# A head's transposes in one row with the weighted sum of one head and the scores of another

## The chip, the cores and the metric

The kernel runs on one core of one Trainium2 chip. The metric is the device time of one execution in microseconds (us). Its engines are PE (TensorE: matmuls, with PEld for its weight loads), DVE (VectorE), ACT (ScalarE), POOL (GpSimd) and SP (SyncE, which only issues transfers here). Each takes its own instructions in the order in which they were written for it.

## The reference, cut to what matters

Two layers. Each has four token mixers, three of them attention with four heads of 64, then gates and branch projections, an output projection and a squared-ReLU MLP. The part around the change:

```
h = rms_norm(x, g_mix)
(a_q, a_k, a_v, b_qlat, ..., c_f, d_val, d_gate) = split(h @ w_in)
out_a = chunk_band_attention(a_q, a_k, a_v, rel_bias)          # 4 heads
out_b = block_causal_attention(q, k, v, CHUNK)                 # 4 heads
out_c = block_causal_attention(c_q, c_k, c_v, 1, f_cum)        # 4 heads
out_d = silu(layer_norm(conv(d_val * sigmoid(d_gate))))
proj  = einsum('bsnc,ncd->bsnd', branches, w_branch)
gates = sigmoid(h @ w_gate + b_gate).reshape(b, s, 4, D_MODEL)
x = x + sum(gates * proj, axis=2) @ w_o
x = x + square(relu(rms_norm(x) @ w_up)) @ w_down
```

256 tokens, width 1024, everything in float32. A head's attention is softmax(q k + bias) v.

## The kernel before

Every float32 weight tile (128 x 1024, 512 KB) is loaded by SP, cast to a high part on ACT (`hi`, line 114) and its rest is taken on DVE or POOL (`lo`, line 115); a product is then three matmuls (lines 122 to 124: high by high, low by high, high by low). One such tile against 256 tokens is 24 matmuls of 256 columns. DVE, ACT and POOL get their order from a scheduler; PE's order is that in which the code is written (line 86).

The twelve heads of a layer (mixer A heads 0 to 3, B 4 to 7, C 8 to 11) are not a stage of their own. Their pieces stand between weight tiles of the projections and the gates: `mtile` ends in `tick()`, and each tick takes the next list of `side` and runs it. For PE a head has three pieces. `scores` (S, line 555) is two products of 128 and 256 columns in plain float32; heads of mixer A have a stationary operand of 64 rows, those of B and C of 128. `transposes` (pT, line 582) turns the three 128 x 128 blocks of the normalised probabilities, which ACT copies out as `pts`. `weighted` (pPV, lines 593 and 594) is again 256 and 128 columns, with a stationary operand of 64 columns. A piece of another kind in this stretch is `pf` (lines 471 and 472, the forget sums), with the columns of an S. The profile shows each plain float32 matmul twice, as two passes.

In `plan` head i has its scores at tick 4 + 2i, its transposes three ticks and its weighted sum four ticks after them. So even ticks hold a weighted sum and a scores, odd ticks a transposes alone. The ticks go on through the projections (0 to 12) into the loop over the 16 gate groups, `gates(g)`, of two tiles (two ticks) each. While `side` still holds a list, that loop does nothing but gates, and every second `lo` goes to POOL (`share[1] = 2`). The first group at whose end `side` is empty takes `conv_silu` and `sigmoids(0)`; each group behind it is followed by one `branch(m)`, and what is left of the eight branches stands behind the last group.

A branch is one weight tile, 24 matmuls of 0.12 us, into two banks of PSUM (`pbr`); DVE multiplies each by the gates (`yt`, line 737), POOL adds in two steps (lines 738 and 739), ACT casts the sum to `yh` (line 740) and DVE takes the rest `yl` (line 741). Behind the branches comes the output projection: four accumulators `po`, in the same four banks that `pgt` and `pbr` go round in, six matmuls each per weight tile and pair of banks, in the order po[0,0], po[1,0] (first tile), po[0,1], po[1,1] (second tile).

Of the kernel before, what the change touches and what calls it, by code (L numbers as in the profile page):

```python
# [47 lines left out]
A0 = 4  # L48
# [22 lines left out]
def hybrid_trunk(ctx: ExitStack, tc: tile.TileContext, xT, xtok, pos, small, gfin, abias, w_lat, w_v, w_in, w_uq, w_ukv,  # L71
# [253 lines left out]
    for l in range(L):  # L325
# [346 lines left out]
            tick()  # L672


        NH = 3 * HEADS
        NT = A0 + 2 * NH + 3
        plan = [[] for _ in range(NT)]
        for i in range(NH):
            plan[A0 + 2 * i].append((2, scores, i))
            plan[A0 + 2 * i + 3].append((1, transposes, i))  # L680
            plan[A0 + 2 * i + 4].append((0, weighted, i))
        side = [[(lambda f=f, i=i: f(i)) for _, f, i in sorted(p, key=lambda e: e[0])] for p in plan]
        side[0].append(lambda: latents(share[2]))
        if l == 0:
# [283 lines left out]
```

## Time and profile before

| what | value |
|---|---|
| median of 3 runs | 844.85 us (843.68 to 844.89) |
| profiled execution, span | 845.43 us, 843.6 us |
| granted PE clock over the span | 0.996 of full |
| busy PE, DVE, ACT, POOL | 826.0, 569.9, 450.0, 152.7 us |
| chain that ended last | PE 89%, DVE 5%, issue 2%, POOL 1%, ACT 1% |
| L114 ACT cast `hi`, mean | 1024 ns |

Busy time says how long an engine had an instruction in it; the chain follows the last instruction back to what released each step. A PE start is a better measure than a PE duration, since matmuls overlap: the starts of gate matmuls stand 0.12 us apart while each lasts 0.28 us.

### The profile page before, as it was taken

To read this page: it belongs to the slowest core of one execution; us is meant where nothing else is said; L and a number is where in the kernel's file an instruction comes from. 1 tells how busy PE (TensorE), PEld (TensorE's weight loads), DVE (VectorE), ACT (ScalarE), POOL (GpSimd) and SP (SyncE) were. 2 spreads that over 40 slices of the span, in tenths; PEclk is the share of its full clock that TensorE was granted. 3 is DMA by queue.
4 is the path that set the end of the run, shared out by engine and by line. 5 is a ranking of instruction groups with operands and counts; after the bars stand their busy time and mean duration, and the time that the engine had idled before them with its cause. 6 is when DMAs were issued, how large, how long until landed. Compare 5 with 4: busy or idle time off the path is not lost.

```text
span 843.6 us, 14520 instructions
## 1 busy us (share of the span) xinstructions
PE 826.0 (98%) x5646; PEld 759.5 (90%) x5646; DVE 569.9 (68%) x950; ACT 450.0 (53%) x759; POOL 152.7 (18%) x156
## 2 busy tenths in 40 slices
PE   9989999999999999999999999999999999999996
PEld 8969999999889999999899899999998899999994
DVE  7889984787665555555578899557866655555554
ACT  6745646654464444544485764485445554545443
POOL 6524332124200000000004332312331000000000
PEclk9999999999999999999999999999999999999999
DMA  8655433555546555555554544345555555555531
GB/s 281 232 181 181 132 126 126 166 184 185 165 164 198 189 189 186 186 189 187 172 176 161 188 132 145 132 131 174 194 176 200 175 186 190 191 185 186 188 126 50
DMA packets 42549, 145.55 MB, mean 173 GB/s; under 512 B 5104, under 2 KB 7408, under 8 KB 42352
## 3 DMA queue, kind: packets, MB, share of 16 engines
q1 hardware_dynamic: 41904, 142.98, 52.1%
q10 hardware_dynamic: 576, 1.64, 0.5%
q8 instruction: 44, 0.72, 0.4%
q14 instruction: 25, 0.20, 0.1%
HBM read 143.55 MB, written 1.05 MB: 171 GB/s over the span
## 4 chain that ended last, share of the span: by engine, by line
PE 89%; DVE 5%; issue 2%; POOL 1%; ACT 1%; DMA 0%; SPq 0%; POOLq 0%; DVEq 0%; ACTq 0%
PE pgt L122 7%; PE pgt L123 7%; PE pgt L124 7%; PE pu L123 7%; PE pu L124 7%; PE pu L122 7%; PE pd L123 7%; PE pd L122 7%; PE pd L124 7%; PE S L555 2%; DVE lo L115 2%; PE pqk L122 2%; PE pPV L593 2%; PE pqk L123 2%; PE pqk L124 2%
## 5 line engine op out<-in xcount | busy, mean ns | idle before, releaser
L115 DVE TENSOR_TENSOR lo<-raw,hi 128x1024 fp32r<-128x1024 f32 (+3 forms) x241 | 300.5, 1250 | 195.9 <-ACT hi L114 193.9
L114 ACT CAST hi<-raw 128x1024 fp32r<-128x1024 f32 (+2 forms) x273 | 278.5, 1024 | 266.0 <-issue 208.0
L122 PE MATMUL pgt<-xgh,hi 128*128 128x256 f32 x512 | 149.5, 292 | 0.0
L122 PE MATMUL pu<-xgh,hi 128*128 128x256 f32 x512 | 144.9, 283 | 0.7 <-ACT xgh L293 0.7
L123 PE MATMUL pu<-xgl,hi 128*128 128x256 f32 x512 | 145.1, 283 | 0.3
L124 PE MATMUL pu<-xgh,lo 128*128 128x256 f32 x512 | 144.9, 283 | 0.0
L123 PE MATMUL pgt<-xgl,hi 128*128 128x256 f32 x512 | 144.7, 283 | 0.0
L124 PE MATMUL pgt<-xgh,lo 128*128 128x256 f32 x512 | 144.7, 283 | 0.0
L122 PE MATMUL pd<-hi,u 128*128 128x512 f32 x256 | 100.8, 394 | 1.6 <-ACT u L803 1.6
L123 PE MATMUL pd<-hi,u 128*128 128x512 f32 x256 | 100.7, 393 | 1.1 <-DVE u L804 1.1
L122 PEld LDWEIGHTS pu<-xgh,hi 128*128 128x128 f32 x512 | 98.0, 191 | 3.4 <-ACT xgh L293 1.1
L123 PEld LDWEIGHTS pu<-xgl,hi 128*128 128x128 f32 x512 | 98.0, 191 | 3.0 <-DVE xgl L294 0.7
L124 PE MATMUL pd<-lo,u 128*128 128x512 f32 x256 | 99.6, 389 | 0.0
L122 PEld LDWEIGHTS pgt<-xgh,hi 128*128 128x128 f32 x512 | 97.9, 191 | 0.8 <-issue 0.3
L123 PEld LDWEIGHTS pgt<-xgl,hi 128*128 128x128 f32 x512 | 98.1, 192 | 0.4
L124 PEld LDWEIGHTS pu<-xgh,lo 128*128 128x128 f32 x512 | 98.0, 191 | 0.0
L124 PEld LDWEIGHTS pgt<-xgh,lo 128*128 128x128 f32 x512 | 97.9, 191 | 0.0
L115 POOL TENSOR_TENSOR lo<-raw,hi 128x1024 fp32r<-128x1024 f32 (+1 forms) x32 | 77.4, 2419 | 111.2 <-ACT hi L114 106.5
L491 DVE SCALAR_TENSOR_TENSOR cacc<-up,sm,cacc 128x256 f32<-128x256 f32 x120 | 77.9, 693 | 0.0
L122 PEld LDWEIGHTS pd<-hi,u 128*128 128x128 f32 x256 | 48.3, 189 | 10.8 <-ACT u L803 2.4
L124 PEld LDWEIGHTS pd<-lo,u 128*128 128x128 f32 x256 | 48.1, 188 | 10.4
L123 PEld LDWEIGHTS pd<-hi,u 128*128 128x128 f32 x256 | 48.3, 189 | 9.7 <-DVE u L804 2.0
(255 smaller groups left out, 1358.3 us busy)
## 6 DMA issues: line engine op xcount, KB each, us to landing
raw<-in_w_gate SPq DMA_DIRECT2D x64, 512.0 KB, 3.7
raw<-in_w_up SPq DMA_DIRECT2D x64, 512.0 KB, 4.2
raw<-in_w_dn SPq DMA_DIRECT2D x64, 512.0 KB, 4.2
raw<-in_w_in SPq DMA_DIRECT2D x23, 512.0 KB, 4.2
raw<-in_w_br SPq DMA_DIRECT2D x16, 512.0 KB, 3.7
raw<-in_w_o SPq DMA_DIRECT2D x16, 512.0 KB, 4.3
raw<-in_w_v SPq DMA_DIRECT2D x8, 512.0 KB, 4.2
raw<-in_w_lat SPq DMA_DIRECT2D x8, 210.0 KB, 4.6
```

The source lines that it names most:

```text
L114: cut = nc.scalar.copy(hi[:, c:c + w], raw[:, c:c + w])
L115: done = eng.tensor_tensor(lo[:, c:c + w], raw[:, c:c + w], hi[:, c:c + w], op=ALU.subtract)
L122: nc.tensor.matmul(ps, sh, mh, start=first, stop=False)
L123: nc.tensor.matmul(ps, *((sl, mh) if late_mov else (sh, ml)), start=False, stop=False)
L124: nc.tensor.matmul(ps, *((sh, ml) if late_mov else (sl, mh)), start=False, stop=last)
L491: ins = nc.vector.scalar_tensor_tensor(cacc[:, c, :], up[:, c, j:j + T], wcol, cacc[:, c, :], op0=ALU.mult, op1=ALU.add)
L555: nc.tensor.matmul(sl, q[:, b * P:(b + 1) * P], k[:, 0:n], start=True, stop=True)
L593: nc.tensor.matmul(po[o:o + 64, 0:T], v[:, 0, vo:vo + HD], pts[:, 0:T], start=True, stop=False)
```

## The change

The transposes of a head move from three to four ticks behind its scores, and its weighted sum from four to six. Both are now on even ticks; within a tick the sum of head i stands first, then the transposes of head i + 1, then the scores of head i + 3. The list of ticks is two longer.

```
         NH = 3 * HEADS
-        NT = A0 + 2 * NH + 3
+        NT = A0 + 2 * NH + 5
         plan = [[] for _ in range(NT)]
         for i in range(NH):
             plan[A0 + 2 * i].append((2, scores, i))
-            plan[A0 + 2 * i + 3].append((1, transposes, i))
-            plan[A0 + 2 * i + 4].append((0, weighted, i))
+            plan[A0 + 2 * i + 4].append((1, transposes, i))
+            plan[A0 + 2 * i + 6].append((0, weighted, i))
```

On PE, in the first layer among the gates, before (the numbers tell the heads' tiles apart; left out are the gate matmuls between):

```order
L582 MATMUL pT_1234<-ident,pe_1083 128x128 x3
...
L593 MATMUL pPV_1273<-pts_1238,VB_383 64x256
L594 MATMUL pPV_1273<-pts_1238,VB_383 64x128
L555 MATMUL S_1276<-qkB_380 128x128
L555 MATMUL S_1276<-qkB_380 128x256
```

and now, the same head's sum and its successor's transposes:

```order
L593 MATMUL pPV_1355<-pts_1271,VB_383 64x256
L594 MATMUL pPV_1355<-pts_1271,VB_383 64x128
L582 MATMUL pT_1358<-ident,pe_1187 128x128 x3
L555 MATMUL S_1364<-qkB_380 128x128
L555 MATMUL S_1364<-qkB_380 128x256
```

Three transposes have moved from between two weight tiles into the row of the sum and the scores.

On DVE, at the end of the first layer's branches, before (yt_2524 is branch 5, yt_2629 branch 6, yt_2672 branch 7, Z_1099<-pgt_2561 the last gates, lo_2713 and on the weights of the output projection):

```order
L741 TENSOR_TENSOR yl_1992<-yt_2524,yh_1991 128x256
L115 TENSOR_TENSOR lo_2713<-raw_2711,hi_2712 128x1024
L717 TENSOR_TENSOR Z_1099<-pgt_2561,rb_465 128x512
L115 TENSOR_TENSOR lo_2731<-raw_2729,hi_2730 128x1024
L737 TENSOR_TENSOR yt_2629<-pbr_2630,Z_1099 128x512
L737 TENSOR_TENSOR yt_2629<-pbr_2644,Z_1099 128x512
L115 TENSOR_TENSOR lo_2749<-raw_2747,hi_2748 128x1024
L741 TENSOR_TENSOR yl_1992<-yt_2629,yh_1991 128x256
L737 TENSOR_TENSOR yt_2672<-pbr_2673,Z_1099 128x512
L737 TENSOR_TENSOR yt_2672<-pbr_2687,Z_1099 128x512
L115 TENSOR_TENSOR lo_2767<-raw_2765,hi_2766 128x1024
L741 TENSOR_TENSOR yl_1992<-yt_2672,yh_1991 128x256
```

and now (yt_2586 is branch 5, yt_2629 and yt_2672 branches 6 and 7 again, Z_1096<-pgt_2518 the last gates):

```order
L718 TENSOR_TENSOR Z_1096<-pgt_2518,rb_465 128x512
L115 TENSOR_TENSOR lo_2713<-raw_2711,hi_2712 128x1024
L738 TENSOR_TENSOR yt_2586<-pbr_2587,Z_1096 128x512
L738 TENSOR_TENSOR yt_2586<-pbr_2601,Z_1096 128x512
L115 TENSOR_TENSOR lo_2731<-raw_2729,hi_2730 128x1024
L742 TENSOR_TENSOR yl_2054<-yt_2586,yh_2053 128x256
L738 TENSOR_TENSOR yt_2629<-pbr_2630,Z_1096 128x512
L738 TENSOR_TENSOR yt_2629<-pbr_2644,Z_1096 128x512
L115 TENSOR_TENSOR lo_2749<-raw_2747,hi_2748 128x1024
L738 TENSOR_TENSOR yt_2672<-pbr_2673,Z_1096 128x512
L742 TENSOR_TENSOR yl_2054<-yt_2629,yh_2053 128x256
L738 TENSOR_TENSOR yt_2672<-pbr_2687,Z_1096 128x512
```

With two ticks more, the first branch stands one gate group later, and behind the last group there are now three branches (5, 6, 7) where there were two (6, 7).

## Rows read from the trace of the kernel before

**Rows 1.** Page, busy us, share and instructions of each engine.

```profile
PE 826.0 (98%) x5646; PEld 759.5 (90%) x5646; DVE 569.9 (68%) x950; ACT 450.0 (53%) x759; POOL 152.7 (18%) x156
```

**Rows 2.** Busy time in a stretch: from:to, length, then each engine.

```profile
80.00:200.00 120.00, 120.00 (x950) 114.86 (x950) 90.99 (x162) 68.61 (x127) 34.41 (x22) 1.00 0.48 152
```

**Rows 3.** PE's waits: us in total, times, longest.

```profile
PE po L122 <- DVE yt L737: 0.6, 2, 0.3
```

**Rows 4.** Timeline of PE, gates, first layer: start us, us, engine line op.

```profile
91.06 0.28 PE L124 MATMUL pgt<-xgh,lo 128*128 128x256 f32 x1
91.27 0.65 PE L593 MATMUL pPV<-pts,VAC 128*64 128x256 f32 x2
...
92.06 0.92 PE L555 MATMUL S<-qkB 128*128 128x128 f32 x4
...
92.94 0.28 PE L123 MATMUL pgt<-xgl,hi 128*128 128x256 f32 x1
...
95.57 0.28 PE L124 MATMUL pgt<-xgh,lo 128*128 128x256 f32 x1
95.69 0.49 PE L582 MATMUL pT<-ident,pe 128*128 128x128 f32 x3
...
96.14 0.28 PE L123 MATMUL pgt<-xgl,hi 128*128 128x256 f32 x1
```

**Rows 5.** Timeline of PE, transposes with the forget sums behind them.

```profile
87.20 0.28 PE L124 MATMUL pgt<-xgh,lo 128*128 128x256 f32 x1
87.32 0.49 PE L582 MATMUL pT<-ident,pe 128*128 128x128 f32 x3
...
88.42 0.28 PE L123 MATMUL pgt<-xgl,hi 128*128 128x256 f32 x1
```

**Rows 6.** Timeline of PE, the gate matmuls around a weighted sum alone.

```profile
153.41 0.28 PE L124 MATMUL pgt<-xgh,lo 128*128 128x256 f32 x1
...
154.64 0.28 PE L123 MATMUL pgt<-xgl,hi 128*128 128x256 f32 x1
```

**Rows 7.** Timeline of PE, mixer A: scores alone, then around sum and scores.

```profile
58.34 0.39 PE L124 MATMUL pv<-lo,xgh 128*128 128x512 f32 x1
58.66 0.92 PE L555 MATMUL S<-qkA 64*128 64x128 f32 x4
...
59.84 0.39 PE L123 MATMUL pv<-hi,xgl 128*128 128x512 f32 x1
...
74.79 0.28 PE L124 MATMUL pqk<-xgh,lo 128*128 128x256 f32 x1
...
76.87 0.28 PE L123 MATMUL pqk<-xgl,hi 128*128 128x256 f32 x1
```

**Rows 8.** Timeline of DVE at the last two branches, first layer.

```profile
215.06 1.28 DVE L737 TENSOR_TENSOR yt<-pbr,Z 128x512 f32<-128x512 f32 x2
216.25 1.21 DVE L115 TENSOR_TENSOR lo<-raw,hi 128x1024 fp32r<-128x1024 f32 x1
219.91 0.43 DVE L741 TENSOR_TENSOR yl<-yt,yh 128x256 fp32r<-128x256 f32 x1 [2.45 <-ACT yh L740]
220.26 1.28 DVE L737 TENSOR_TENSOR yt<-pbr,Z 128x512 f32<-128x512 f32 x2
```

**Rows 9.** Timeline of POOL and ACT, branch 6, first layer.

```profile
216.48 2.14 POOL L738 TENSOR_TENSOR yt<-yt 128x512 f32<-128x512 f32 x1 [5.72 <-DVE yt L737]
218.69 0.75 POOL L739 TENSOR_TENSOR yt<-yt 128x256 f32<-128x256 f32 x1
219.47 0.41 ACT L740 CAST yh<-yt 128x256 fp32r<-128x256 f32 x1 [3.31 <-POOL yt L739]
```

**Rows 10.** Timeline of PE, start of the output projection, first layer.

```profile
217.86 0.40 PE L122 MATMUL po<-hi,yh 128*128 128x512 f32 x1
...
220.38 0.39 PE L124 MATMUL po<-lo,yh 128*128 128x512 f32 x1
221.09 0.47 PE L122 MATMUL po<-hi,yh 128*128 128x512 f32 x1 [0.31 <-DVE yt L737]
```

## The prediction

> **What bounds the kernel now.** I read the busy times first: PE is busy for 826.0 of 843.6 us [rows 1]. Then the stretch in which the heads' pieces stand among the gates: from 80 to 200 us PE is busy for all of 120 us at a granted clock of 1.00, while DVE has 91 and ACT 69 [rows 2]. So a piece of a head costs there what it takes on PE, and what other engines do more or later costs nothing until PE waits for it. Then the list of PE's waits: between the heads and the MLP it has one row, 0.6 us in two waits, one in each layer, where the output projection waits for DVE's products of the last branch [rows 3]. The change touches both: what PE does at the ticks, and how many branches stand in front of the output projection. The sum has these two terms.
>
> **PE at the ticks.** I price a place by the starts of the weight matmuls around it: from the last line 124 before it to the first line 123 behind it, less the two starts that would be there anyway. Gate matmuls start 0.12 us apart (92.94 to 95.57 is 22 starts, 2.63 us) [rows 4].
> - Transposes alone: 96.14 - 95.57 - 0.24 = 0.33 us [rows 4]. They start 0.12 behind the gate matmul, like another gate matmul: the place has no hole at its front.
> - Sum and scores (mixers B, C): 92.94 - 91.06 - 0.24 = 1.64 us [rows 4].
> - Sum alone: 154.64 - 153.41 - 0.24 = 0.99 us [rows 6]. So scores behind a sum add 0.65.
> - Transposes and forget sums: 88.42 - 87.20 - 0.24 = 0.98 us [rows 5]; behind transposes, the same columns as a scores add 0.98 - 0.33 = 0.65 too.
>
> Sum and scores have the same columns, and yet a sum alone takes 0.99 and a scores 0.65. The 0.34 more is the sum's own: its first pass starts 0.21 behind a gate matmul instead of 0.12 (91.06 to 91.27) [rows 4], and the rest, some 0.2 to 0.25, lies behind it. It is there whether a scores or a gate matmul comes next, since the difference of the two places is just the scores. Transposes have the 128 x 128 form of both, so I expect the same hole in front of them and none behind: sum, transposes and scores in a row take 1.64 + 0.33 = 1.97 us, what the two places take now. For the 11 sums per layer that get transposes behind them that is a gain of 0. No row shows transposes behind a sum, so the bounds are these: they fill the hole (-0.2 each, 22 times: -4.4 us) or meet a second one on the way to the scores (+4.4 us). I take 0, since the rows on either side of the new place, sum with scores and transposes with forget sums, both add up without gain or loss.
>
> Mixer A's scores are another form, 64 rows. Alone between matmuls of 512 columns, which start 0.23 apart, such a scores takes 59.84 - 58.34 - 0.46 = 1.04 us, and it starts 0.32 behind its predecessor: holes of its own on both sides [rows 7]. Sum and scores of mixer A together take 76.87 - 74.79 - 0.24 = 1.84 us [rows 7], less than 0.99 + 1.04 = 2.03: the hole between the two odd forms is paid once. Heads 2 and 3 stand behind a sum now. After the change head 2's scores stand behind transposes, and head 3's behind sum and transposes: the shared hole, 0.19 us, is paid separately at both. Two heads, two layers: 4 x 0.19 = +0.8 us. Bounds: 0, if the hole in front of such a scores is not there behind transposes, and 1.2 us with 0.3 each, the whole 0.32 of that start.
>
> The Trainium skill, TensorE: Matmul & The Clock Gate, Part 3 (The mechanism), says that a weight load runs beside matmuls in flight only if its row group differs. The rows differ: loads of full height are busy for 90% of the span beside PE's 98% [rows 1], and it is the 64-row scores that starts late [rows 7]. By the page mixer A's term would be 0 and the sum 1.9 us in place of 2.7.
>
> The two added ticks cost PE nothing by themselves, as the same gate tiles are only counted against other lists. One more `lo` per layer goes to POOL and leaves DVE; PE waits for neither in that stretch. Transposes now stand a tick further behind their scores and sums two ticks behind their transposes, so both find their operands earlier than now.
>
> **The end of the branches.** DVE goes strictly down its list: the products of one branch wait behind `yl` of the branch before, which waits for ACT's cast, which waits for POOL's two adds. From one branch's products to the next that is 220.26 - 215.06 = 5.20 us [rows 8], made of 1.28 for the products, 2.14 and 0.75 on POOL, 0.41 on ACT and 0.43 on DVE [rows 8, 9] and the gaps between. PE needs only 24 x 0.12 = 2.88 us for a branch. Behind gates (5.76 us and a branch) the chain fits; branches without gates between run ahead of it. Now there is one such step (6 to 7); it costs PE 221.09 - 220.38 - 0.23 = 0.48 us of which the profile counts 0.31 as waiting [rows 10]. After the change there are two (5 to 6, 6 to 7).
>
> I take the first-layer times of branch 6, which is the one behind the last gates now, for branch 5, one branch (2.88 us) earlier, so that the output projection is due at 217.86 as it is now [rows 10]. Products of 5 start at 215.06 - 2.88 = 212.18. Products of 6 start 5.20 later at 217.38; the first is done at 218.06 (0.68), the second at 218.66. The first accumulator takes the bank of the first product, which PE sees 0.15 us after its end (220.94 to 221.09 in [rows 8, 10]): 218.21, a wait of 0.35. Then DVE does a weight tile (1.21, to 219.8) and the first product of 7 (to 220.5), in time for the third accumulator at 218.21 + 12 x 0.229 = 220.96. But the second product of 7 stands behind `yl` of 6 in the new order: POOL starts at 218.8 and is done at 221.75, ACT at 222.2, `yl` at 222.65, the product at 223.3, PE sees it at 223.4. The fourth accumulator is due six matmuls after the third, at 222.33: a wait of 1.1. Together 1.45 us, against 0.48 now: +0.95 us per layer, +1.9 us for both, since the waits of the two layers are alike [rows 3]. Bounds: 0, if PE comes late enough by other delays, and two whole steps of 5.20 - 2.88 = 2.32, less the 0.48 paid now, 4.2 per layer, if nothing of the chain were covered.
>
> **Sum.** 843.6 + 0.8 + 1.9 = 846.3 us of span; with the 1.83 us that the profiled execution has around its span (845.43 - 843.6) 848.1 us. The median of the runs lies 0.58 below the profiled one, so I predict 844.85 + 2.7 = 847.6 us.
>
> **Rivals.**
> - The transposes fill the sum's hole, and the kernel is not slower. Price: 22 x 0.2 = 4.4 us, 847.6 - 4.4 = 843.2 us; from 0.05 us per place on (1.0 us in all) the change is no longer measurable as slower. For it: the hole is there [rows 4, 6] and the transposes would be the first thing of that size behind it. Against: the hole is as long in front of a gate matmul as in front of a scores.
> - The end of the branches costs nothing, because PE waits 1.45 us only if DVE starts branch 5's products as early behind the gates as it now starts branch 6's; what is left is mixer A: 844.85 + 0.8 = 845.7 us, no difference to be seen. For it: a wait on PE in one place often takes away another's. Against: the list of waits has none behind it that it could take away.
> - The chain holds up the weights too. ACT casts the fifth tile of the output projection behind branch 7's `yh`, which by the working above ends at 223.3 + 0.13 + 2.96 + 0.44 = 226.8; cast and `lo` (1.02 and 1.21) are done at 229.0. PE starts this tile at 217.86 + 4 x 2.75 + 1.45 = 230.3, so 1.3 us are left; if the chain is longer by more than that, PE waits. With 0.6 us a layer this gives 848.8 us.
>
> **How the numbers follow.** The forecast 0.60, the filled hole 0.12, the covered end 0.20, held-up weights 0.08. About 0.2%, 1.7 us, is what a measurement can tell from no change: slower begins at 846.5. The forecast's own range, 846.4 to 848.8, is nearly all above it, and with the last rival gives 0.62 for slower. No change: the covered end, half of the filled hole and the lower edge of the forecast, 0.28. Faster: 0.10, the better half of the filled hole and something for the bound of -4.4 with a covered end. The range goes from 844.0, inside the filled hole's case, to 849.3 above the held-up weights; the bounds of +-4.4 lie outside at both ends.
>
> **What would show it.** Around a row of sum, transposes and scores, 2.21 us (1.97 + 0.24) from the last line 124 to the first line 123: 2.0 would be the filled hole, 2.4 a second one. Mixer A's row of head 3: 0.99 + 0.33 + 1.04 + 0.24 = 2.60 us. In PE's waits the row of `po` grows from 0.6 to about 2.5 us in four waits. I am wrong on the main point if that row does not grow, or if PE gets waits between 80 and 200 us.

## The result and the profile after

The kernel after the change takes 851.75 us (median of 4 runs, 851.23 to 852.75), the kernel before 844.87 us (843.68 to 845.21). The ratio is 1.0085, with an interval of 1.0068 to 1.0103: slower by 6.9 us, where 2.7 was forecast and 849.3 us was the end of the range. The profiled execution is the lowest of its four runs, 851.23 us, with a span of 849.4 us and a granted clock of 0.996 as before; the spans differ by 5.8 us, and it is this that the profile can account for.

The page's busy times after the change, to be read beside [rows 1]:

```profile
PE 826.8 (97%) x5646; PEld 758.4 (89%) x5646; DVE 583.5 (69%) x948; ACT 448.7 (53%) x759; POOL 158.9 (19%) x158
```

PE runs as many instructions for almost the same time. DVE has two instructions fewer and is busy for 13.6 us more. That is the line to stop at: an engine that does less and takes longer.

PE's waits after the change, the main rows that are new or changed (us in total, times, longest):

```profile
PE pPV L593 <- DVE brl L598: 2.8, 4, 1.0
PE S L555 <- DVE qkA L636: 1.9, 1, 1.9
PE po L122 <- DVE yt L738: 1.7, 3, 0.8
...
PE pb L278 <- DVE rh L269: 1.1, 2, 0.5
...
PE pqk L124 <- POOL lo L115: 0.7, 1, 0.7
```

The third row is the one that was forecast, 0.6 before [rows 3]. The first and the fourth stand in the stretch of the heads, where PE had no wait before [rows 2]: a head's sum waits until DVE has read the sum of the pair before it (`brl`) out of the one bank that `pPV` has, and `pb`, a product for the convolution's scale, waits for its operand `rh`. The second row lies in front of 62 us, and before the change it was the longest of all:

```profile
PE S L555 <- DVE qkA L636: 3.3, 1, 3.3
```

**The rows that were priced.** PE's timeline after the change at head 3's row of mixer A, which answers to [rows 7], and at a row of mixer B that does not wait, which answers to [rows 4]:

```profile
73.33 0.28 PE L124 MATMUL pqk<-xgh,lo 128*128 128x256 f32 x1
73.54 0.65 PE L593 MATMUL pPV<-pts,VAC 128*64 128x256 f32 x2
...
74.33 0.55 PE L582 MATMUL pT<-ident,pe 128*128 128x128 f32 x3
74.81 0.92 PE L555 MATMUL S<-qkA 64*128 64x128 f32 x4
...
75.88 0.28 PE L123 MATMUL pqk<-xgl,hi 128*128 128x256 f32 x1
...
97.39 0.28 PE L124 MATMUL pgt<-xgh,lo 128*128 128x256 f32 x1
97.60 0.65 PE L593 MATMUL pPV<-pts,VAC 128*64 128x256 f32 x2
...
98.39 0.55 PE L582 MATMUL pT<-ident,pe 128*128 128x128 f32 x3
98.77 0.82 PE L555 MATMUL S<-qkB 128*128 128x128 f32 x4
...
99.55 0.28 PE L123 MATMUL pgt<-xgl,hi 128*128 128x256 f32 x1
```

Sum, transposes and scores cost 99.55 - 97.39 - 0.24 = 1.92 us, against 1.97 in two places before: 0.05 us less in each of the 20 rows of this kind (all but mixer A's), 1.0 us in all. Head 3's row costs 75.88 - 73.33 - 0.24 = 2.31 us. With head 2's, transposes and scores alone at 1.37, mixer A costs 0.33 us more per layer than before, 0.7 us in both.

**The end of the branches.** DVE's timeline at branches 5, 6 and 7 and PE's at the second tile of the output projection, first layer, which answer to [rows 8] and [rows 10]:

```profile
213.93 1.28 DVE L738 TENSOR_TENSOR yt<-pbr,Z 128x512 f32<-128x512 f32 x2
...
219.37 1.28 DVE L738 TENSOR_TENSOR yt<-pbr,Z 128x512 f32<-128x512 f32 x2
...
221.70 0.68 DVE L738 TENSOR_TENSOR yt<-pbr,Z 128x512 f32<-128x512 f32 x1
224.22 0.42 DVE L742 TENSOR_TENSOR yl<-yt,yh 128x256 fp32r<-128x256 f32 x1 [1.83 <-ACT yh L741]
224.56 0.68 DVE L738 TENSOR_TENSOR yt<-pbr,Z 128x512 f32<-128x512 f32 x1
...
225.30 0.50 PE L122 MATMUL po<-hi,yh 128*128 128x512 f32 x1 [0.75 <-DVE yt L738]
```

The second product of branch 7 stands behind `yl` of branch 6, and PE's fourth accumulator waits for it. From the first matmul of branch 7 to the third tile of the projection it is 9.77 us (217.02 to 226.79) where it was 8.95: 0.82 more per layer, 1.6 us in both.

**The new waits.** All three engines around one of the four waits for `brl`:

```profile
100.86 2.48 POOL L115 TENSOR_TENSOR lo<-raw,hi 128x1024 fp32r<-128x1024 f32 x1 [3.54 <-ACT hi L114]
101.00 3.42 DVE L491 SCALAR_TENSOR_TENSOR cacc<-up,sm,cacc 128x256 f32<-128x256 f32 x3
104.35 0.68 DVE L718 TENSOR_TENSOR Z<-pgt,rb 128x512 f32<-128x512 f32 x1
...
105.06 0.28 PE L124 MATMUL pgt<-xgh,lo 128*128 128x256 f32 x1
105.34 0.41 DVE L598 TENSOR_TENSOR brl<-pPV,brh 128x256 fp32r<-128x256 f32 x1
...
105.90 0.62 PE L593 MATMUL pPV<-pts,VB 128*64 128x256 f32 x2 [0.56 <-DVE brl L598]
```

and `brl` of the same pair in the kernel before:

```profile
93.81 0.42 DVE L598 TENSOR_TENSOR brl<-pPV,brh 128x256 fp32r<-128x256 f32 x1
```

Before, `brl` starts 2.5 us after its sum (91.27 in [rows 4]); after, 7.7 us after it (97.60 to 105.34), and the next sum, due at 105.3, has to wait. Some 3.5 us of this (2.5 before) pass until ACT has cast `brh`, the other operand; from then on DVE is not waiting, it is late. The taps of the convolution are its multiply-adds, one per place of the filter and half of the channels, on DVE. The three of line 491 at 101.00 take 3.42 us where one takes 0.47: the first starts 0.14 us after POOL has begun a weight tile and ends at 103.63, 0.3 us behind POOL's end (103.34). The four waits cost 0.60 and 1.03 us in the first layer and 0.34 and 1.0 in the second, 3.0 us.

The other new wait, first layer, POOL, DVE and PE:

```profile
148.33 2.40 POOL L115 TENSOR_TENSOR lo<-raw,hi 128x1024 fp32r<-128x1024 f32 x1
148.40 2.35 DVE L269 CAST rh<-rc 128x2 fp32r<-128x2 f32 x1 [0.83 <-POOL rc L266]
150.90 0.30 PE L278 MATMUL pb<-identr,rh 128*128 128x128 f32 x1 [0.55 <-DVE rh L269]
```

and the same cast before:

```profile
148.08 0.17 DVE L269 CAST rh<-rc 128x2 fp32r<-128x2 f32 x1 [0.23 <-POOL rc L266]
```

A cast of two columns takes 2.35 us in place of 0.17. POOL's tile at 148.33 is the second of gate group 9, which is POOL's only because the list of ticks is two longer. The place of `pb` costs 0.79 us more in each layer, 1.6 in both.

DVE's groups of instructions show most of it, the taps and `rh` after, then the taps before (busy us, mean ns):

```profile
L491 DVE SCALAR_TENSOR_TENSOR cacc<-up,sm,cacc 128x256 f32<-128x256 f32 x120 | 90.1, 793 | 0.0
...
L269 DVE CAST rh<-rc 128x2 fp32r<-128x2 f32 x4 | 5.0, 1262 | 3.1 <-POOL rc L266 3.1
```

```profile
L491 DVE SCALAR_TENSOR_TENSOR cacc<-up,sm,cacc 128x256 f32<-128x256 f32 x120 | 77.9, 693 | 0.0
```

15 of the 120 taps took over 1 us before, 19 after, most of these the whole 2.6. Held taps were there before; from 80 to 200 us they cost nothing that PE saw, and the prediction did not take them one by one.

| term, us | forecast | measured |
|---|---|---|
| rows of sum, transposes, scores | 0 | -1.0 |
| mixer A's scores | +0.8 | +0.7 |
| end of the branches | +1.9 | +1.6 |
| waits for `brl` | 0 | +3.0 |
| wait for `rh` | 0 | +1.6 |
| in front of the first `puq` (62.6 to 62.0 us, of which 0.3 is a transposes that now comes later) | 0 | -0.3 |
| sum | +2.7 | +5.6, of a span longer by 5.8 |

### The profile page after: what moved, and what is told of

It is laid out like the page before. It is cut to its first block, busy times and chain, and to the rows that moved or that the text cites. A ratio compares the mean times of both kernels' runs of the same rounds, so it can differ in the third digit from the quotient of the medians.

```text
span 849.4 us, 14514 instructions
## 1 busy us (share of the span) xinstructions
PE 826.8 (97%) x5646; PEld 758.4 (89%) x5646; DVE 583.5 (69%) x948; ACT 448.7 (53%) x759; POOL 158.9 (19%) x158
## 4 chain that ended last, share of the span: by engine, by line
PE 77%; DVE 14%; issue 3%; ACT 2%; POOL 2%; DMA 1%; SPq 0%; POOLq 0%; ACTq 0%; DVEq 0%
PE pu L123 7%; PE pu L124 7%; PE pu L122 7%; PE pd L123 7%; PE pd L122 7%; PE pd L124 7%; DVE cacc L491 6%; PE pgt L122 5%; PE pgt L123 4%; PE pgt L124 4%; DVE lo L115 3%; PE po L122 1%; PE pqk L122 1%; PE po L124 1%; PE po L123 1%
## 5 line engine op out<-in xcount | busy, mean ns | idle before, releaser
L115 DVE TENSOR_TENSOR lo<-raw,hi 128x1024 fp32r<-128x1024 f32 (+3 forms) x239 | 294.9, 1237 | 189.8 <-ACT hi L114 188.5
L115 POOL TENSOR_TENSOR lo<-raw,hi 128x1024 fp32r<-128x1024 f32 (+1 forms) x34 | 83.6, 2461 | 102.3 <-ACT hi L114 88.6
L491 DVE SCALAR_TENSOR_TENSOR cacc<-up,sm,cacc 128x256 f32<-128x256 f32 x120 | 90.1, 793 | 0.0
```

The source lines that it names most:

```text
L115: done = eng.tensor_tensor(lo[:, c:c + w], raw[:, c:c + w], hi[:, c:c + w], op=ALU.subtract)
L491: ins = nc.vector.scalar_tensor_tensor(cacc[:, c, :], up[:, c, j:j + T], wcol, cacc[:, c, :], op0=ALU.mult, op1=ALU.add)
```

## The experiments

The theory: DVE's taps and casts are held while POOL runs a weight tile; after the change more of them are, DVE falls behind, and PE meets this in two places. The rivals: the waits belong to the new row of three pieces, or to the shorter way between `pc` and `pb`, or to a new order on DVE, which the scheduler makes afresh for every edit. Each edit is shown against the kernel after the change unless the text names another.

**POOL takes no weight tile while the heads run**, after the change and, beside it, before it:

```
-        share[1] = 2
+        share[1] = 0
```

> The changed kernel, but no weight rest (lo) goes to POOL while the heads' pieces run: all stand on DVE. Theory 1 (DVE is held): a convolution tap that starts on DVE while POOL takes a lo is held until POOL ends (2.6 us in place of 0.47), this happens 19 times among the taps after the change, DVE falls a period behind, and PE waits for brl and for rh. Without a lo on POOL the taps go back to 0.47 us, and PE's waits for brl (2.8 us) and rh (1.1 us by the profile, 1.6 by the starts) go: 851.75 - 3.0 - 1.6 = 847.2 us. Theory 2 (DVE simply has too much to do or in a worse order): 26 lo of 1.23 us more on DVE are 32 us more work in the stage, the waits for brl grow, the time is 852 us or more.

Measured: 842.28 us, ratio to the kernel before 0.9965 (0.9951 to 0.9978): 9.5 us less than with the change as it is, twice what was expected. No wait for `brl` or `rh` is left, with the wait for `po` still at 1.7. DVE's taps, and the first matmuls of the query projection (`puq`; us of the first and last start) in the kernel after and in this one:

```profile
L491 DVE SCALAR_TENSOR_TENSOR cacc<-up,sm,cacc 128x256 f32<-128x256 f32 x120 | 52.7, 475 | 0.0
```

```profile
L122 PE MATMUL puq<-lath,hi x16: 277/283/283, 62.0 to 478.3; 128*128 128x256 f32 x16
```

```profile
L122 PE MATMUL puq<-lath,hi x16: 277/283/284, 57.8 to 471.7; 128*128 128x256 f32 x16
```

No tap is held, though DVE now has all the `lo` (34 more, not the 26 that were expected). From the first `puq` to the end it is 840.6 - 57.8 = 782.8 us against 849.4 - 62.0 = 787.4: 4.6 us less, which is the 3.0 and 1.6 of the table. The other 4.2 us lie in front of 62 us, a stretch that the expectation had not priced. The next run shows what they are.

> The kernel before, with no lo on POOL while the heads' pieces run. Theory 1: its 17 held taps go too and DVE's taps fall from 81 to 58 us, but PE waits for DVE nowhere in that stretch, so the time stays: 844.9 us. Theory 2: 26 lo more on DVE make PE wait, 846 us or more.

Measured: 840.64 us, ratio 0.9946 (0.9931 to 0.9961), where no change was expected. The rows of the kernel before that explain it, POOL, DVE and PE around 45 us, then its stretches from 40 to 60 us (length, PE, PEld, DVE, ACT, POOL, granted clock):

```profile
41.86 2.42 DVE L488 TENSOR_SCALAR cacc<-up,sm 128x256 f32<-128x256 f32 x2
44.20 3.39 DVE L491 SCALAR_TENSOR_TENSOR cacc<-up,sm,cacc 128x256 f32<-128x256 f32 x3
44.75 2.57 POOL L115 TENSOR_TENSOR lo<-raw,hi 128x1024 fp32r<-128x1024 f32 x1 [0.94 <-ACT hi L114]
...
49.44 0.74 DVE L636 TENSOR_TENSOR qkA<-pqk,rb 128x256 f32<-128x256 f32 x2
49.91 0.92 PE L555 MATMUL S<-qkA 64*128 64x128 f32 x4 [3.29 <-DVE qkA L636]
```

```profile
40.00:50.00 10.00, 6.71 (x46) 5.88 (x45) 10.00 (x12) 3.89 (x5) 6.38 (x3) 1.00 0.51 156
50.00:60.00 10.00, 10.00 (x40) 7.55 (x41) 6.96 (x22) 5.40 (x11) 1.53 (x3) 0.83 0.63 221
```

and the same stretches without POOL's tiles:

```profile
40.00:50.00 10.00, 10.00 (x63) 8.56 (x62) 9.83 (x22) 6.09 (x9) 0.23 (x2) 1.00 0.73 251
50.00:60.00 10.00, 10.00 (x56) 8.16 (x55) 9.56 (x25) 7.07 (x17) 0.23 (x2) 1.00 0.68 214
```

The first scores wait 3.29 us for `qkA`, which stands on DVE behind held instructions (the first pair of line 488 takes 2.42 us for 0.73 without POOL's tiles). PE is idle for 3.29 of these ten us, and in the next ten the granted clock is 0.83: for part of the time it was at 1.2 GHz instead of 2.4, 0.17 x 10 = 1.7 us lost. Both are gone without POOL's tiles, 5.0 us against 4.7 by which the first `puq` comes earlier (62.6 to 57.9 us); behind it both kernels take 781.0 us. The held instructions cost the kernel before too, but at its start. The spread of the runs goes with POOL's tiles as well: each of the five kernels without POOL's tiles varies by 0.3 to 0.6 us, each of the others by 1.4 to 4.7 us. The change's price without any hold is 842.28 - 840.64 = 1.6 us, against -1.0 + 0.7 + 1.6 = 1.3 in the table.

**One weight tile taken from POOL, and POOL's tiles in halves**:

```
         for g in range(16):
+            if g == 9:
+                share[1] = 0
             gates(g)
```

> The changed kernel, but the lo of the second tile of gate group 9 stands on DVE, as it does before the change: one lo per layer leaves POOL. Theory 1: the cast rh, held 2.35 us by exactly this lo, takes 0.17 us, PE's wait for rh goes, 0.79 us per layer, 851.75 - 1.6 = 850.2 us; the wait for brl stays. Rival: PE waits for rh because no transposes stand between pc and pb any more (0.65 us less distance); then the wait stays and the time is 851.8 us.

Measured: 849.24 us, ratio 1.0046 (1.0030 to 1.0061). That is 2.5 us less than with the change as it is, where 1.6 was expected. The wait for `rh` is gone, the cast takes 169 ns again, and the waits for `brl` stay (2.6 us, four). The order on PE is the same, so the way from `pc` to `pb` is not the cause: one instruction of POOL is.

```
-            done = eng.tensor_tensor(lo[:, c:c + w], raw[:, c:c + w], hi[:, c:c + w], op=ALU.subtract)
+            h = w if eng is nc.vector else w // 2
+            for d in range(c, c + w, h):
+                done = eng.tensor_tensor(lo[:, d:d + h], raw[:, d:d + h], hi[:, d:d + h], op=ALU.subtract)
```

> The changed kernel, but each lo that goes to POOL is taken there in two halves of 512 columns. Theory 1 (a tap that starts while POOL runs is held until that POOL instruction ends): no tap takes longer than 0.47 + 1.3 = about 1.8 us, where 2.6 us is usual now; the sum of the taps falls from 90.1 us towards 70, the waits for brl (2.8 us) fall to under 1.5, 849.5 us. Rival (a tap is slow for another reason, such as its place in the list): single taps still take 2.6 us and the time stays at 851.8.

Measured: 848.85 us, ratio 1.0048 (1.0033 to 1.0063). Two taps on DVE and the two halves on POOL beside them (the lines of this kernel are numbered two higher):

```profile
95.01 1.91 DVE L493 SCALAR_TENSOR_TENSOR cacc<-up,sm,cacc 128x256 f32<-128x256 f32 x2
...
95.21 2.87 POOL L117 TENSOR_TENSOR lo<-raw,hi 128x512 fp32r<-128x512 f32 x2 [8.21 <-ACT hi L114]
```

The second tap takes 1.5 us, as 30 of the 33 held taps of this run do, the length of one half and not of both, so it is the single instruction on POOL that holds it. But 33 taps are held for over 1 us in place of 19; their sum falls to 85.4 us, not towards 70, and the mean only to 753 ns. The waits for `brl` are gone. PE, ACT and DVE run the same instructions in the same order as in the kernel after, which no other edit of POOL's share leaves so; only POOL's instructions are cut in two. So it is the length of a hold that brings the wait for `brl`, and not a new order on DVE. The wait of `pb` stays at 1.1 us: each half now holds one of its two operands, `rh` for 1.26 us and `rlo` for 1.20. The first `puq` comes 1.1 us later than in the kernel after, since the wait for `qkA` is 2.7 us there and the clock from 50 to 60 us 0.72.

**POOL takes the other tile of each pair**:

```
+        share[0] += l == 0
         share[1] = 2
```

> The kernel after the change, in which POOL takes the other weight tile of every pair in the stretch of the heads: PE's order, the plan of the heads and the number of POOL's weight tiles (within one) stay. Theory: the new waits of PE (2.8 us for brl, 1.1 us for rh) come from which instructions of DVE start while POOL runs a weight tile, so they change or go when POOL's tiles come at other times; with none of them the time is 851.75 - 3.0 - 1.6 = about 847.1 us, and the mean of a tap falls from 793 ns to under 700. Rival: the waits belong to the new row of sum, transposes and scores itself, and stay whichever tiles POOL takes: 851 to 852 us, brl still 2.5 us or more.

The edit shifts the count by which every second tile goes to POOL.

Measured: 848.76 us, ratio 1.0055 (1.0035 to 1.0074); the profiled execution is the slowest of six, with 849.5 us of span. Its wait for `qkA`, its first `puq` and PE's stretch from 50 to 60 us (length, PE, clock):

```profile
PE S L555 <- DVE qkA L636: 4.9, 1, 4.9
```

```profile
L122 PE MATMUL puq<-lath,hi x16: 278/283/283, 66.6 to 480.4; 128*128 128x256 f32 x16
```

```profile
50.00:60.00 10.00, 7.34 (x23) 0.66 0.56 189
```

The waits for `brl` and `rh` are gone, as the theory had it; the mean of a tap fell only to 764 ns, not below 700. Behind the first `puq` it takes 849.5 - 66.6 = 782.9 us, just what it takes with no tile on POOL (782.8). In this execution what is won there is lost in front, where other instructions are held now; the median of the six runs is 3.0 us below the kernel after, of the 4.6 that were expected. The row of three pieces is the same here and does not wait: that rival falls. The scheduler has given DVE another order here, so this run alone would not tell the hold from the order; the run with halves does.

**Half of the change.** The shared row with short distances (transposes two ticks, sums four ticks behind the scores), then the long distance of the sums alone:

```
-        NT = A0 + 2 * NH + 5
+        NT = A0 + 2 * NH + 3
-            plan[A0 + 2 * i + 4].append((1, transposes, i))
-            plan[A0 + 2 * i + 6].append((0, weighted, i))
+            plan[A0 + 2 * i + 2].append((1, transposes, i))
+            plan[A0 + 2 * i + 4].append((0, weighted, i))
```

> Transposes two and weighted sums four ticks behind their scores: the shared row as in the change, but no longer list of ticks; POOL takes its weight tiles as before. The end of the branches then costs what it did before (0.6 us of waits for po), mixer A's rows cost about 0.9 us more than before and the rows of the other heads 1.0 us less. If the waits for brl and rh come with the longer distances and the phase that they give DVE, they are gone here: 844.8 us. If the shared row brings them, brl costs 3 us here too: 847.8 us.

Measured: 845.31 us, ratio 1.0008 (0.9997 to 1.0019): as fast as before. No wait for `brl` or `rh`, 13 taps over 1 us.

```
-            plan[A0 + 2 * i + 4].append((1, transposes, i))
+            plan[A0 + 2 * i + 3].append((1, transposes, i))
```

> Transposes stay alone on the odd ticks, three behind their scores; only the weighted sum moves, to six ticks, with the list two ticks longer. The end of the branches costs 1.6 us more than before, mixer A's rows and the other rows nothing or little. If the waits for brl and rh come with the longer distances, they are here as in the change: 844.9 + 1.6 + 3.0 + 1.6 = 851 us. If the shared row brings the waits for brl, only rh can stay: 846.5 to 848 us.

Measured: 849.30 us, ratio 1.0054 (1.0033 to 1.0075). PE's wait is there, at half its size:

```profile
PE pPV L593 <- DVE brl L598: 1.4, 2, 0.7
```

From a sum's second pass to `brl` it is up to 7.7 us (7.9 in the change), and `rh` is held. So the six ticks bring DVE's lag beside POOL's tiles, without the shared row; with the shared row the waits that follow from it are twice as long. Why DVE's order then lets taps start at the front of POOL's tiles, where before they started later in them, no run separates.

**One branch earlier**, so that two and not three stand behind the last gates, with POOL's tiles and without:

```
-            if side:
+            if len(side) > 2:
                 continue
-            share[1] = 0
+            if not side:
+                share[1] = 0
```

> The changed kernel, but the branches start one gate group earlier, as they do before the change (the last sum then stands right in front of branch 0): two branches instead of three behind the last gates. By the term for the end of the branches PE's wait for po falls from 1.7 to 0.6 us and the output projection starts 0.82 us earlier per layer: 851.75 - 1.6 = 850.1 us, or up to 1 us more if branch 0 now waits for the last sum's brl. If that term does not come from the number of branches, 851.8 us.

Measured: 850.06 us, ratio 1.0054 (1.0036 to 1.0071). The wait for `po` is 0.6 us again. The edit also moved the cast `rh` out from under POOL's tile, so it is no clean test of the one term: behind the first `puq` it takes 784.7 us, 2.7 less than the kernel after, where the two terms of the table would give 3.2, and the median fell by 1.7.

> The changed kernel with no lo on POOL in the heads' stretch (842.28 us, 1.64 us over the kernel before with the same edit) and with the branches starting one gate group earlier. By the term for the end of the branches the wait for po falls from 1.7 to 0.6 us and the time by 2 x 0.82 us: 840.6 us, the kernel before with the same edit (840.64). If the difference between the two lies in the pieces' places on PE instead, 842.3 us.

Measured: 841.52 us, ratio 0.9959 (0.9947 to 0.9972), 0.8 us less than without POOL's tiles alone, half of what was expected. `po` waits 0.6 us, but `pb` now waits for `rlo` (0.7 us in two).

**A version from the findings**: short distances, no tile on POOL, and then mixer A's transposes in front of the sum.

> No lo on POOL in the heads' stretch, and the transposes two ticks, the sums four ticks behind their scores: the same rows of sum, transposes and scores as after the change, with as many ticks as before, so the branches start as early as before. By the starts measured after the change, 11 rows per layer gain 0.046 us each and mixer A loses 0.35 us per layer: 840.64 - 1.0 + 0.7 = 840.3 us. If two ticks are too few for the softmax, PE gets waits for pe and it is 841 us or more.

Measured: 840.49 us, ratio 0.9947 (0.9934 to 0.9959), as expected, and as the kernel before does without POOL's tiles: the shared row gains nothing that can be measured.

And against the kernel just measured:

```
-            plan[A0 + 2 * i + 2].append((1, transposes, i))
+            plan[A0 + 2 * i + 2].append((-1 if i + 1 < HEADS else 1, transposes, i))
```

> As the last one, but where the scores of the row are of mixer A the transposes stand in front of the sum, so that sum and scores share the hole between their two forms again: 2 rows per layer, 0.15 to 0.2 us each, 0.7 us in all: 839.6 us. If the hole is not shared, 840.3 us.

Measured: 839.97 us, ratio 0.9940 (0.9927 to 0.9954), the fastest here. Mixer A's row in it:

```profile
70.06 0.28 PE L124 MATMUL pqk<-xgh,lo 128*128 128x256 f32 x1
70.18 0.49 PE L582 MATMUL pT<-ident,pe 128*128 128x128 f32 x3
70.60 0.65 PE L593 MATMUL pPV<-pts,VAC 128*64 128x256 f32 x2
...
72.46 0.28 PE L123 MATMUL pqk<-xgl,hi 128*128 128x256 f32 x1
```

72.46 - 70.06 - 0.24 = 2.16 us against 2.31 with the sum first: the hole that the 64-column sum and the 64-row scores share is paid once again.

## Why the prediction was wrong

What the sum priced, mixer A and the end of the branches, came out within 0.3 us each, and the rows put at 0 within 1.0. The step that failed is the paragraph on the two added ticks, which put what DVE does among the heads at nothing. There the change cost 4.6 us, 3.0 in waits for `brl` and 1.6 in the wait for `rh`, since POOL's weight tiles hold instructions of DVE.

- **"what other engines do more or later costs nothing until PE waits for it"** is true as it stands; the fault is that I took the time left beside DVE's 91 of 120 busy us [rows 2] as slack, so that PE would never have to wait, without reading single instructions. And the list of PE's waits had a longer row than the one I took for the only one between the heads and the MLP [rows 3]: the 3.3 us for `qkA`, ahead of the gates but among the heads, and behind held instructions of DVE too. The mean of a tap, 693 ns, stood on the page, beside single taps of 0.47 us. 15 taps of more than 1 us, each beside a weight tile on POOL, would have said that DVE's time there hangs on when POOL starts.
- **"One more `lo` per layer goes to POOL and leaves DVE; PE waits for neither in that stretch"** is where it fails for `rh`. The change moved a tile off DVE, and on POOL that tile held the cast `rh`: 1.6 us. I had priced whom the tile waits for, not whom it holds.
- **"both find their operands earlier than now"** holds for operands. The sum waits for a bank, which DVE has to read first. With six ticks and POOL's tiles `brl` came 7.7 us behind its sum and not 2.5: 3.0 us. With six ticks and no tile on POOL it comes 1.4 to 2.9 us behind, so the ticks alone are not the cause. With one bank, DVE has the time from one sum to the next and no more to read it, and that limit belonged in the working.
- **The end of the branches** was right: the wait, its instruction and its cause (second product of 7 behind `yl` of 6), at 1.6 us for 1.9. It shows as three waits, 1.7 us, not four and 2.5.
- **Mixer A** was right at 0.7 for 0.8: head 3's row is 2.55 us from start to start for the 2.60 named, and the price of the 64-row form is paid again as the rows said.
- **The transposes behind a sum** cost 0.05 us less than apart, not 0.2 as in the rival and not 0: -1.0 us in all, which hid part of the rest.
- The mark set for being wrong, waits of PE between 80 and 200 us, is what came. The one rival on the slow side, held-up weights, lies at the end of the branches; none named DVE's work among the heads.

The Trainium skill, SBUF — State Buffer, section "SBUF: two separate sides", bears on this, and I had not weighed it: DVE and POOL share a pair of ports, and an instruction of DVE with two SBUF inputs (only against one of POOL that reads SBUF), or in a two-port mode, or of POOL, whichever is first, keeps it to its end ("an exclusive lock, not a bandwidth split"). The rows agree for the taps (2.6 us held, 0.47 alone), and for the halves on POOL (1.5 us). The cast of `rh` has one input and was held as well; whether it was in such a mode, no run here shows.

## What to carry to other kernels

When a change shifts two engines against each other, busy shares are not slack: look for a group whose mean is well above its shortest instruction, and see what ran on the other engine at the long ones. Price a moved instruction by what it holds as well as by what waits for it; here a tile taken off the busier engine made that engine later. And where a fault of this kind turns up, take it out of the kernel before as well: most of the gain of the fastest version here (ratio 0.9940), 4.6 us (ratio 0.9946), had nothing to do with the change.

## What the hardware showed that I had not expected

- Some instructions of DVE that start while POOL runs a `lo` of 1024 columns are held to its end: a tap of 0.47 us takes up to 2.7, a cast of two columns 2.35 in place of 0.17. Others are not: `brl`, which reads PSUM for one of its inputs, had a mean of 421 ns before, when 8 of 12 ran beside such a tile, and of 416 after, when 2 did; and the reciprocal of the softmax's sums, which has one input of two columns in SBUF, takes 0.17 us beside a tile as alone.
- Giving DVE all of POOL's tiles made DVE's taps take 52.7 us in place of 90.1, and the kernel faster by 9.5 us after the change and 4.6 before it.
- Behind a wait of PE of 3.3 us the granted clock was 0.83 in the next ten us, 1.7 us more; beside a wait of 4.9 us, which began before 50 us and ended behind it, it was 0.66 from 50 to 60 us. The length of the wait does not settle it alone: behind one of 2.5 us the clock stayed at 1.00 with the short distances, and was 0.83 with the branches one group earlier. The first of these two executions, at 843.15 us, is the fastest of its kernel's ten.
